# A PEER expert mixer on one Trainium2 core: the second row block's choices moved among the dense blocks, dot products among the queries, two rings for the query weights

## The chip, the cores and the metric

The kernel runs on one core of one Trainium2 chip. The core has five engines, each with its own in-order queue of instructions: TensorE (PE in the profile; its weight loads are listed apart as PEld), VectorE (DVE), ScalarE (ACT), GpSimd (POOL) and SyncE (SP), which here only issues DMAs. The metric is the device time of one execution in microseconds (us), lower is better; a kernel's time is the median of its runs. A profile shows one execution, and its span runs from the first to the last instruction.

## The reference

One decoding step of a hybrid layer: an input projection feeds an RWKV-7 head group and a sparse-attention head group, whose outputs are projected, added to the input and normed. Then comes the part that the change touches, a PEER mixer: for every token and each of 8 heads, two halves of a query are scored against 128 subkeys each, the best 16 of either half are combined, the best 16 of the combinations name 16 of 16384 experts, and each chosen expert adds its row of `v_tab`, weighted by a gate and by the gelu of the dot product of the token with the expert's row of `u_tab`. There are 256 prompt tokens and 32 sample tokens, D = 2048, all in float32.

```python
q = (xt @ wq).reshape(n, P_HEADS, 2, P_DKEY // 2)
s = jnp.einsum('nhcd,hckd->nhck', q, subkeys).astype(jnp.float32)
hv, hix = lax.top_k(s, P_TOPK)
cand = (hv[:, :, 0, :, None] + hv[:, :, 1, None, :]).reshape(n, P_HEADS, P_TOPK * P_TOPK)
cand_e = (hix[:, :, 0, :, None] * N_KEYS + hix[:, :, 1, None, :]).reshape(n, P_HEADS, P_TOPK * P_TOPK)
tv, tpos = lax.top_k(cand, P_TOPK)
expert = jnp.take_along_axis(cand_e, tpos, axis=-1)
gate = jax.nn.softmax(tv, axis=-1).astype(x.dtype)
h = jax.nn.gelu(jnp.einsum('cd,chkd->chk', xb, u_tab[eb]), approximate=False)
return jnp.einsum('chk,chkd->cd', gb * h, v_tab[eb])
```

## The kernel before

The kernel is written against a layer that records instructions in program order, allots tiles in on-chip memory, adds the semaphores, and orders each engine's queue by a planner: it simulates the run and lets each engine take, of the instructions that are ready in the simulation, the one that stands first in the program. So an instruction can be queued earlier than its place in the text, and what the planner took for ready is waited for on the chip. `tc.issue_after(x)` holds the instructions inside it behind `x` on the queue of `x`'s engine. Tiles come from pools that are stacked from the left and from the right end of the memory; a pool that is closed gives its place to later ones, whose tiles wait until the old tile there is no longer used. A tile name with `bufs=n` is a ring of n places.

The 256 prompt tokens are two row blocks of 128, `t` = 0 and 1. From the first norm on (lines 1716 to 1756), in program order:

- **Norm.** The rows X1 are normed, turned into `XT` for TensorE, multiplied and shifted, and written to DRAM as `X1D` by four DMAs of GpSimd (line 1752).
- **Query stage** (lines 1762 to 1857). For head `h` TensorE multiplies `XT` with the query weights of two column groups `c` (32 loads of 512 KB through one ring, `wraw`, of four tiles; line 1711), ScalarE copies the result to `QP`, TensorE scores both row blocks against the subkeys, and ScalarE copies the scores to `TB`, where four tiles take turns (line 1383). `choose` (line 1386) then finds the best on VectorE, with the sums of indices and a masked product (lines 1394, 1400, 1411) on GpSimd; `settle` reduces the masked product to 16 indices of experts, a head later, which GpSimd writes to `GI[t]`. Dot products of the 32 sample tokens (`late`, line 1556; two gathers of 512 KB a token) run in between on VectorE. At `h == 2` SP loads the first 896 columns of the normed rows back, `X1a[t]` (line 1829).
- **Dense blocks** (lines 1854 to 1876). The dot product of token and expert is split by columns. For the last 1152 columns TensorE forms all 128 x 128 experts' products in 128 blocks `i1`: nine float32 matmuls each, 18 instructions in the profile, on weights `ur` of 576 KB (ring of five), into five PSUM banks `ph`, from which ScalarE copies to `AW`. For the first 896 columns only the chosen experts are formed: per pair of row block and choice one gather of 448 KB by GpSimd into `rows` (ring of five) and one multiply-and-sum by VectorE into a column of `HD[t]` (line 1794), 256 in all, two a block in program order. These are the *dots*. `gates` (softmax of the chosen scores, an exponential on ScalarE) stands ahead of the blocks for both row blocks, and `table(0)`, which turns indices, gates and `HD` of the first row block for the next stage, at 152 dots.
- **Weigh stage** (lines 1879 to 2012), 64 steps that read `AW` and `TB`; `table(1)` stands at step 20. The ring `rows` also takes the sample tokens' gathers of this stage.
- **V stage** (line 2016 on), the weighted sum of the experts' rows of `v_tab`, then the last norm. The first load of its table, line 1971, stands at step 50 of the weigh stage.

## Time and profile before

| what | value |
|---|---|
| time, median of three runs (lowest to highest) | 2457.12 us (2453.75 to 2460.82) |
| the profiled execution's own time | 2451.44 us |
| its span | 2449.7 us |
| TensorE / VectorE / ScalarE / GpSimd busy, share of the span | 92% / 71% / 33% / 54% |
| mean granted TensorE clock | 0.95 |
| DMA over the span | 684.09 MB, mean 279 GB/s |

A row of the costliest groups reads: line, engine, operation, output<-input, shapes, count, then busy us and mean ns of one, then the engine's idle time ahead of them and what ended it. A row of the timeline reads: start and length in us, engine, line, operation, output<-input, shapes, count, and in brackets the idle time before it with what ended it; equal neighbours are merged. Matmuls overlap, so the mean duration of one is longer than the distance from one to the next. An SPq row in the view of waits gives what SP's queue waited for: us in total, times, the longest.

### The profile page before, as it was taken

The page shows a single profiled execution, that of the slowest core. Times are in us where ns is not written, and L with a number is a line of the kernel's source. Part 1 is how long each engine was busy: PE and PEld are TensorE (multiplying, and loading weights), DVE is VectorE, ACT ScalarE, POOL GpSimd, SP SyncE. Part 2 cuts the span into 40 slices and gives each one's busy share as a digit, 9 for nine tenths or more (in the row PEclk, how much of TensorE's full clock was granted, in tenths as well). Part 3 has the DMA queues.
Part 4 walks back from the last instruction along what each step waited for, and adds up shares of the span by engine and source line. Part 5 has one row for each costly group of instructions (what it writes and reads, how often), then busy time and mean ns, then how long its engine had stood idle before and what let it go on. Part 6 is the DMA issues. An engine that isn't in the chain of part 4 may idle for free.

```text
span 2449.7 us, 42718 instructions
## 1 busy us (share of the span) xinstructions
PE 2254.7 (92%) x15628; PEld 1886.4 (77%) x15628; DVE 1748.2 (71%) x3985; ACT 819.9 (33%) x1591; POOL 1332.6 (54%) x1419
## 2 busy tenths in 40 slices
PE   7989999997988997779989999998998999999996
PEld 7977898884645665568878888887777888887885
DVE  5789766555653456789955555556777799998888
ACT  4433223223431333220111111111777544444343
POOL 5678423233445003567757555666442688876762
PEclk9999999998996996999999999999999999999998
DMA  7887975448668984988499999998664799999994
GB/s 221 233 247 224 281 213 167 136 141 261 213 228 250 312 277 160 320 287 271 147 402 399 400 403 388 390 400 313 190 190 131 280 359 365 357 369 361 353 346 187
DMA packets 327602, 684.09 MB, mean 279 GB/s; under 512 B 82270, under 2 KB 200992, under 8 KB 326464
## 3 DMA queue, kind: packets, MB, share of 16 engines
q1 hardware_dynamic: 246176, 342.58, 42.1%
q0 software_dynamic: 81216, 338.78, 38.4%
q8 instruction: 123, 2.02, 0.3%
q14 instruction: 87, 0.71, 0.1%
HBM read 665.69 MB, written 23.88 MB: 281 GB/s over the span
## 4 chain that ended last, share of the span: by engine, by line
PE 51%; issue 13%; DVE 12%; POOL 11%; DMA 9%; ACT 2%; SPq 1%; POOLq 0%; DVEq 0%; ACTq 0%
PE pb L2066 20%; POOL rows L454 9%; PE pj L423 8%; PE pa L1660 3%; PE px L1904 3%; PE pa L1937 2%; DVE sr L1556 2%; PE p L1080 2%; PE pt L1896 2%; DMA co<-in_cache_cmp_kv,gidx 2%; PE ss L1497 1%; DMA rows<-in_peer_u_g,gi 1%; PE fs L1955 1%; DVE CA L477 1%; DMA co<-in_cache_sel_kv,sidx 1%
## 5 line engine op out<-in xcount | busy, mean ns | idle before, releaser
L1867 PE MATMUL ph<-Xfd,ur 128*128 128x256 f32 x2304 | 500.8, 380 | 10.1 <-DMA ur<-in_peer_u_t 9.7
L1867 PEld LDWEIGHTS ph<-Xfd,ur 128*128 128x128 f32 x2304 | 439.2, 191 | 71.0 <-issue 10.0
L454 POOL DMA_INDIRECT rq<-in_peer_v_g,gi x256 | 377.6, 1475 | 153.2 <-DVE fP L2039 88.4
L1794 DVE SCALAR_TENSOR_TENSOR rows<-rows,x1a 128x896 f32<-128x896 f32 x256 | 282.0, 1103 | 197.0 <-DMA rows<-in_peer_u_g,gi 195.9
L454 POOL DMA_INDIRECT rows<-in_peer_u_g,gi x256 | 293.1, 1145 | 184.8 <-DVE rows L1794 152.8
L423 PE MATMUL pj<-XH,wl 128*128 128x288 f32 (+1 forms) x752 | 232.2, 309 | 11.3 <-DVE wl L418 6.4
L423 PE MATMUL pj<-XH,wh 128*128 128x288 f32 (+1 forms) x752 | 230.4, 306 | 13.0 <-DVE ss L753 5.9
L2039 DVE SCALAR_TENSOR_TENSOR fP<-rq,ge,fP 128x640 f32<-128x640 f32 x254 | 223.7, 881 | 7.8 <-DMA rq<-in_peer_v_g,gi 5.5
L423 PE MATMUL pj<-XL,wh 128*128 128x288 f32 (+1 forms) x752 | 226.6, 301 | 0.0
L1868 ACT COPY AW<-ph 128x256 f32<-128x256 f32 x128 | 77.0, 609 | 405.9 <-PE ph L1867 400.2
L2066 PE MATMUL pb<-vl,ah 128*128 128x512 f32 (+1 forms) x768 | 207.0, 378 | 0.8
L2066 PE MATMUL pb<-vh,al 128*128 128x512 f32 (+1 forms) x768 | 205.3, 375 | 0.0
L2066 PE MATMUL pb<-vh,ah 128*128 128x512 f32 (+1 forms) x768 | 186.7, 378 | 13.4 <-ACT vh L2058 10.9
L416 ACT CAST wh<-wraw 128x512 fp32r<-128x512 f32 (+1 forms) x188 | 114.6, 616 | 224.1 <-PE pj L423 178.5
L2066 PEld LDWEIGHTS pb<-vh,ah 128*128 128x128 f32 x768 | 144.8, 195 | 35.7 <-ACT vh L2058 13.9
L477 DVE SCALAR_TENSOR_TENSOR CA<-co,wbc,CA 128x256 f32<-128x256 f32 x248 | 135.9, 586 | 49.7 <-DMA co<-in_cache_cmp_kv,gidx 49.7
L2066 PEld LDWEIGHTS pb<-vl,ah 128*128 128x128 f32 x768 | 144.9, 195 | 23.0 <-DVE vl L2059 3.8
L423 PEld LDWEIGHTS pj<-XH,wl 128*128 128x128 f32 (+1 forms) x752 | 144.4, 192 | 22.4 <-DVE wl L418 9.1
L2066 PEld LDWEIGHTS pb<-vh,al 128*128 128x128 f32 x768 | 145.0, 194 | 19.4
L423 PEld LDWEIGHTS pj<-XH,wh 128*128 128x128 f32 (+1 forms) x752 | 144.9, 193 | 19.4 <-DVE ss L753 6.4
L423 PEld LDWEIGHTS pj<-XL,wh 128*128 128x128 f32 (+1 forms) x752 | 144.9, 193 | 1.5 <-issue 1.2
L418 DVE TENSOR_TENSOR wl<-wraw,wh 128x512 fp32r<-128x512 f32 (+1 forms) x141 | 100.2, 720 | 40.0 <-ACT wh L416 39.8
(844 smaller groups left out, 4331.4 us busy)
## 6 DMA issues: line engine op xcount, KB each, us to landing
ur<-in_peer_u_t SPq DMA_DIRECT2D x128, 576.0 KB
wraw<-in_w_in SPq DMA_DIRECT2D x152, 256.0 KB
cw<-in_w_out SPq DMA_DIRECT2D x32, 512.0 KB
wraw<-in_w_out SPq DMA_DIRECT2D x32, 512.0 KB
wraw<-in_peer_wq SPq DMA_DIRECT2D x32, 512.0 KB
cw<-in_peer_wq SPq DMA_DIRECT2D x32, 512.0 KB
wraw<-in_w_in SPq DMA_DIRECT2D x64, 128.0 KB
co<-in_state_win_kv SPq DMA_DIRECT2D x16, 512.0 KB
```

The costliest lines, as they stand in the source:

```text
L416: sc.copy(wh[:, :, :n], w[:, :, :n])
L418: i_ = en.tensor_tensor(wl[:, :, :n], w[:, :, :n], wh[:, :, :n].bitcast(F32), OP.subtract)
L423: last[2] = pe.matmul(pb[:n, :nt], wi[:, k, :n], xi[(o + k) // 8][:, (o + k) % 8, :nt], start=(o + k == 0 and wi is wh and xi is xh), stop ...
L454: gp.indirect_dma_start(out=dst, out_offset=None, in_=rows_, in_offset=bass.IndirectOffsetOnAxis(ap=ix, axis=0))
L477: ve.scalar_tensor_tensor(d_, x_, w_, d_, op0=OP.mult, op1=OP.add)
L1660: pe.matmul(acc[t], xi[:, e, P * t:P * t + P], wi[:, e, :], start=(k == e == n_ == 0), stop=(k == 6 and e == 1 and n_ == 2))
L1794: i_ = ve.scalar_tensor_tensor(r_, r_, 1.0, X1a[t], op0=OP.mult, op1=OP.mult, accum_out=h_)
L1867: mm = pe.matmul(ph[:, :NPR], w[:, e, :], Xfd[:, e, :], start=(e == 0), stop=(e == NDB - 1))
L1868: return mm, sc.copy(AW[:, i1 // 64, :, i1 % 64], ph[:, :NPR])
L1904: pin(pe.matmul(px[:, 128 * e:128 * e + 128].rearrange("p (c j) -> p c j", c=2), oT[:, e, :], AW[:, :, 4 * u + e, :], start=True, stop=True))
L2039: ve.scalar_tensor_tensor(fP[t], r_, w_, fP[t], op0=OP.mult, op1=OP.add)
L2066: pe.matmul(acc[3 * t + q][:, :n_], wi[:, P * t:P * t + P], xi[:, 512 * q:512 * q + n_], start=(k == 0 and wi is ah and xi is vh), stop=(k ...
```

## The change

Five constants change: `NDW` (dots per head in the query stage) from 1 to 5, `NCB` = 10 is new, `ND` and `NDN` go.

- In the query stage `choose` runs for row block 0 alone. Its scores go to `TB[:, h % 4]`; those of row block 1 go to a new tile `S1` with a place for every head. From `h` = 3 on, five dots follow each head (30 in all) where one followed each of the last two.
- The choices of row block 1 are made by a new generator `choose_parts`, six parts a head, drawn among the dense blocks at six parts per ten blocks, behind the last dot so far on VectorE. All of its work is on VectorE, but for the copy of the indices to `GI[1]`, which is ScalarE's. `gates(1)` follows at block 80, `table(0)` moves to block 90.
- The dots that are left are spread evenly over the 128 blocks.
- Query weights come through two rings of four tiles, `wraw` and `wraw2`. The load of `X1a[0]` stands behind the 13th weight load on SP's queue, that of `X1a[1]` and the dense weights behind the last.
- `QP` is a ring of six tiles of one column group each. `rows` moves to a pool `rp` of its own with tiles of 896 columns, closed before the weigh stage, which has its own ring `rows`. The order of the pools on the left becomes `up`, `rp`, `dp` (with `S1`), `kc`, `kq`.

```diff
-NDW = 1
-ND = 1
-NDN = 8
+NDW = 5
+NCB = 10
...
-        S = TB[:, (2 * h + t) % 4].rearrange("p (a b) -> p a b", a=2) if t < 2 else pool([P, 2, P], "S")
+        S = (TB[:, h % 4], S1[:, h])[t].rearrange("p (a b) -> p a b", a=2) if t < 2 else pool([P, 2, P], "S")
...
+    def choose_parts(h, pool, S, TV):
+
+        HV, HI, HF = (pool([P, 2, 16], nm, ty) for nm, ty in (("HVb", F32), ("HIb", U32), ("HFb", F32)))
+        for c in range(2):
+            top16(S[:, c, :], HV[:, c, :], HI[:, c, :])
+            yield 1
+        for c in range(2):
+            ve.tensor_scalar(HF[:, c], HI[:, c], 1.0 if c else 1.0 * P, 0.0, op0=OP.mult, op1=OP.add)
+        CV, CE = (pool([P, NCAND], nm) for nm in ("CVb", "CEb"))
+        for dst, src in ((CV, HV), (CE, HF)):
...
+        yield 1
+        TI, TF = (pool([P, 16], nm, ty) for nm, ty in (("TIb", U32), ("TFb", F32)))
+        top16(CV, TV[:, h, :], TI)
+        ve.tensor_copy(TF, TI)
+        yield 1
+        hit = rp([P, UG], "rows", bufs=NRW)[:, :16 * NCAND].rearrange("p (a b) -> p a b", a=16)
+        ve.tensor_tensor(hit, iota[:, None, :NCAND].to_broadcast([P, 16, NCAND]),
+                         TF[:, :, None].to_broadcast([P, 16, NCAND]), OP.is_equal)
+        ve.tensor_tensor(hit, hit, CE[:, None, :].to_broadcast([P, 16, NCAND]), OP.mult)
+        yield 1
+        EF = pool([P, 16], "EFb")
+        ve.tensor_reduce(EF, hit, AX.X, OP.add)
+        sc.copy(GI[1][:, 16 * h:16 * h + 16], EF)
+        yield 1
...
-        w = wring()
-        sy.dma_start(w, w_q[:, 128 * c:128 * c + 128].rearrange("(k p) c -> p k c", p=P)[:, o:o + 8])
+        w = wring() if c == 0 or o else kq([P, 8, P], "wraw2", bufs=4)
+        wl_.append(sy.dma_start(w, w_q[:, 128 * c:128 * c + 128].rearrange("(k p) c -> p k c", p=P)[:, o:o + 8]).ins)
...
+    rp([P, UG], "rows", bufs=NRW)
+    S1 = dp([P, 8, 2 * P], "S1")
...
-        if h == 2:
-            for t in range(2):
+        if h in (3, 8):
+            with tc.issue_after(wl_[12 if h < 8 else -1]):
+                t = h // 8
                 sy.dma_start(X1a[t], X1D[P * t:P * t + P, :UG])
         if h:
             late_, hits = hits, []
-            for t in range(2):
-                chosen, hit = choose(t, h - 1, kc, S[t], TV[t])
-                hits.append(hit)
+            chosen, hit = choose(0, h - 1, kc, S[0], TV[0])
+            hits.append(hit)
...
-                if h > 6:
+                if h > 2:
                     dot(NDW, 16 * (h - 1), ahead=2)
...
-    for t in range(2):
-        gates(t, up, TV[t])
+    gates(0, up, TV[0])
...
-        sy.dma_start(w.rearrange("p k e -> p (k e)"), a["peer_u_t"][P * i1:P * i1 + P, :])
+        with tc.issue_after(wl_[-1]):
+            sy.dma_start(w.rearrange("p k e -> p (k e)"), a["peer_u_t"][P * i1:P * i1 + P, :])
...
+    later, early = seq(*(choose_parts(h, kc, S1[:, h].rearrange("p (a b) -> p a b", a=2), TV[1]) for h in range(8))), got[1]
     for i1 in range(P):
         mm, end = dense(i1)
-        n_ = ND + (i1 * NDN % 8 < NDN)
-        dot(min(max(P - got[1], 0) or n_, n_))
-        if got[1] == P + 24:
+        n_ = early + -(-(2 * P - early) * (i1 + 1) // P)
+        dot(n_ - got[1])
+        with tc.issue_after(last_dot[0].ins):
+            for _ in take(later, 6 * (i1 + 1) // NCB - 6 * i1 // NCB):
+                pass
+            if i1 == 8 * NCB:
+                for _ in later:
+                    pass
+                gates(1, up, TV[1])
+        if i1 == 8 * NCB + 10:
             with tc.issue_after(mm.ins), tc.issue_after(end.ins):
                 table(0)
     kc.close()
     dp.close()
+    rp.close()
...
+    x4p([P, 1024], "rows", bufs=NRW)
...
-    dot(2 * P - got[1])
```

More of the change, by code (lines that the diff above doesn't have):

```diff
@@ L1374, in scores @@
             if t < 2:
-                pe.matmul(pb[:, 128 * c:128 * c + 128], QP[:, 2 * h + c, P * t:P * t + P], SKT[:, 2 * h + c, :],
+                pe.matmul(pb[:, 128 * c:128 * c + 128], QP[2 * h + c][:, P * t:P * t + P], SKT[:, 2 * h + c, :],
                           start=True, stop=True)
@@ L1386, in choose @@
     def choose(t, h, pool, S, TV):
-        nb_ = 2 if t < 2 else 1
+        nb_ = 1
         HV, HI, HF = (pool([P, 2, 16], nm, ty, bufs=nb_) for nm, ty in (("HV", F32), ("HI", U32), ("HF", F32)))
@@ L1404, in choose @@
         TI, TF = (pool([P, 16], nm, ty, bufs=nb_) for nm, ty in (("TI", U32), ("TF", F32)))
-        hit = up([P, 1024], "rows", bufs=NRW) if t < 2 else pool([P, 1024], "cw", bufs=NCW)
+        hit = rp([P, UG], "rows", bufs=NRW) if t < 2 else pool([P, 1024], "cw", bufs=NCW)
         hit = hit[:, :16 * NCAND].rearrange("p (a b) -> p a b", a=16)
@@ L1412, in choose @@
         return i_, hit
+    def choose_parts(h, pool, S, TV):
[7 more added lines that the diff above has]
+        for dst, src in ((CV, HV), (CE, HF)):
+            o = 0
+            for i0, ni, w in CAND:
+                ve.tensor_tensor(dst[:, o:o + ni * w].rearrange("p (i j) -> p i j", i=ni),
+                                 src[:, 0, i0:i0 + ni, None].to_broadcast([P, ni, w]),
+                                 src[:, 1, None, :w].to_broadcast([P, ni, w]), OP.add)
+                o += ni * w
+        yield 1
[12 more added lines that the diff above has]
+        yield 1
     def settle(t, h, pool, hit):
@@ L1708, in query_load @@
     def query_load(c, o):
-        w = wring()
-        sy.dma_start(w, w_q[:, 128 * c:128 * c + 128].rearrange("(k p) c -> p k c", p=P)[:, o:o + 8])
+        w = wring() if c == 0 or o else kq([P, 8, P], "wraw2", bufs=4)
+        wl_.append(sy.dma_start(w, w_q[:, 128 * c:128 * c + 128].rearrange("(k p) c -> p k c", p=P)[:, o:o + 8]).ins)
         return w
+    wl_ = []
     wq_ = {(0, o): query_load(0, o) for o in (0, 8)}
@@ L1766, in hybrid_decode_step @@
     TV = [up([P, 8, 16], f"TV{t}") for t in range(2)]
-    up([P, 1024], "rows", bufs=NRW)
     xa_ = up([P, 2 * UG], "x1a")
@@ L1770, in hybrid_decode_step @@
     TB = up([P, 4, NPR], "TB")
-    dp, kc, kq = (Pool(nm, "left") for nm in ("dp", "kc", "kq"))
+    rp, dp, kc, kq = (Pool(nm, "left") for nm in ("rp", "dp", "kc", "kq"))
+    rp([P, UG], "rows", bufs=NRW)
+    S1 = dp([P, 8, 2 * P], "S1")
     dp([P, NDB, P], "ur", bufs=NUR)
@@ L1774, in hybrid_decode_step @@
     SKT = kq([P, 16, P], "SKT")
-    QP = kq([P, 16, NPR], "QP")
     dots = [(t, s_) for t in range(2) for s_ in range(P)]
-    got, rows_ = [0, 0], {}
+    got, rows_, last_dot = [0, 0], {}, []
     def fetch(upto):
@@ L1783, in fetch @@
             t, s_ = dots[i]
-            rows_[i] = up([P, 1024], "rows", bufs=NRW)[:, :UG]
+            rows_[i] = rp([P, UG], "rows", bufs=NRW)
             gather(rows_[i], a["peer_u_g"], GI[t][:, s_:s_ + 1])
@@ L1796, in dot @@
                 tc.keep_in_program_order(i_)
-            got[1] = i + 1
+            got[1], last_dot[:] = i + 1, [i_]
     def table(t):
@@ L1802, in table @@
         for q, (op_, v_) in enumerate(((OP.logical_shift_right, 7), (OP.bitwise_and, 127))):
-            ii = up([P, P], "ii", I32, bufs=4)
+            ii = up([P, P], "ii", I32, bufs=2)
             iff = ii.bitcast(F32)
@@ L1815, in hybrid_decode_step @@
     for h in range(9):
-        S = []
+        S, QP = [], {2 * h - 2 + c: q_ for c, q_ in enumerate(QN)} if h else {}
+        QN = [kq([P, NPR], "QP", bufs=6) for c in range(2)]
         for c in (2 * h, 2 * h + 1):
@@ L1823, in hybrid_decode_step @@
                         pe.matmul(pb[:, :NPR], w[:, k, :], XT[:, o + k, :], start=(o + k == 0), stop=(o + k == 15))
-                last_ = sc.copy(QP[:, c, :], pb[:, :NPR])
+                last_ = sc.copy(QN[c % 2], pb[:, :NPR])
             if h and c == 2 * h:
                 S = [scores(t, h - 1, kc, QP, SKT, "pb") for t in range(2)]
-        if h == 2:
-            for t in range(2):
+        if h in (3, 8):
+            with tc.issue_after(wl_[12 if h < 8 else -1]):
+                t = h // 8
                 sy.dma_start(X1a[t], X1D[P * t:P * t + P, :UG])
@@ L1949, in smp_fetch @@
         for q in range(2):
-            sr[j, q] = up([P, 1024], "rows", bufs=NRW)
+            sr[j, q] = x4p([P, 1024], "rows", bufs=NRW)
             gather(sr[j, q], vh2, ig[q][:, j:j + 1])
```

## The prediction

> **What bounds the kernel now.** I read the page's costliest groups first, then TensorE's timeline from the first query matmul to the first matmul of the next stage, then what SP's queue waited for.
>
> ```profile
> L1867 PE MATMUL ph<-Xfd,ur 128*128 128x256 f32 x2304 | 500.8, 380 | 10.1 <-DMA ur<-in_peer_u_t 9.7
> ```
> ```profile
> L1794 DVE SCALAR_TENSOR_TENSOR rows<-rows,x1a 128x896 f32<-128x896 f32 x256 | 282.0, 1103 | 197.0 <-DMA rows<-in_peer_u_g,gi 195.9
> ```
> ```profile
> 1052.18 17.53 PE L1823 MATMUL pj<-XT,wraw 128*128 128x256 f32 x80 [1.89 <-ACT XT L1736]
> ...
> 1089.78 1.22 PE L1375 MATMUL pb<-SKT,QP 128*128 128x128 f32 x4 [4.05 <-ACT QP L1824]
> ...
> 1104.38 13.29 PE L1823 MATMUL pj<-XT,wraw 128*128 128x256 f32 x48 [4.97 <-DMA wraw<-in_peer_wq]
> ...
> 1132.65 13.98 PE L1823 MATMUL pj<-XT,wraw 128*128 128x256 f32 x64
> ...
> 1147.36 13.98 PE L1823 MATMUL pj<-XT,wraw 128*128 128x256 f32 x64
> ...
> 1184.86 27.36 PE L1867 MATMUL ph<-Xfd,ur 128*128 128x256 f32 x126
> 1212.69 11.92 PE L1867 MATMUL ph<-Xfd,ur 128*128 128x256 f32 x54 [0.47 <-ACT AW L1868]
> 1234.27 255.35 PE L1867 MATMUL ph<-Xfd,ur 128*128 128x256 f32 x1170 [9.66 <-DMA ur<-in_peer_u_t]
> ```
> ```profile
> 1497.23 198.73 PE L1867 MATMUL ph<-Xfd,ur 128*128 128x256 f32 x920
> ...
> 1700.28 0.48 PE L1809 MATMUL pb<-CT,hd 128*128 128x128 f32 x1 [3.99 <-DVE rows L1794]
> ...
> 1703.27 2.07 PE L1904 MATMUL px<-AW,oT 128*128 128x128 f32 x8 [0.68 <-ACT oT L1898]
> ```
>
> TensorE is the bound of this stretch, and it is nearly gapless. A head of the query stage costs 1147.36 − 1132.65 = 14.71 us. A dense matmul costs 198.73 / 920 = 0.216 us, so a dense block (18 of them) costs 3.89 us. Eight heads and 2304 dense matmuls need 117.7 + 497.7 = 615.4 us. From 1052.18 that would end at 1667.6; it ended at 1695.96. So 28 us were lost: 4.05 + 4.97 + 0.47 + 9.66 = 19.2 us in four gaps, the rest to a lower clock behind them. Another 7.3 us pass until the first matmul of the weigh stage, 3.99 of them waiting for the last dot product. VectorE has gaps too: its 256 dots wait 195.9 us for gathered rows. In the last 400 us of the dense stage the DMA engines are full:
>
> ```profile
> 1295.00:1695.00 400.00, 400.00 (x1857) 352.09 (x1856) 234.40 (x427) 63.15 (x104) 247.54 (x214) 1.00 1.01 393
> ```
>
> (The columns: stretch and length, then busy time and instructions of TensorE, its weight loads, VectorE, ScalarE and GpSimd, then TensorE's granted clock, the DMA share and GB/s.) So two chains run side by side through the dense blocks and end 4 us apart: TensorE's, and the dots' behind the DMA. Only shortening both moves the end.
>
> **The change part by part.** The causes of the gaps are in what SP's queue and ScalarE waited for; the last two rows are stretches with a low clock:
>
> ```profile
> SPq L1971 <- POOL gi L1418: 19.1, 1, 19.1
> SPq L1829 <- DMA x1d<-x: 11.6, 2, 7.4
> ```
> ```profile
> 1086.62 0.65 ACT L1383 COPY TB<-pb 128x256 f32<-128x256 f32 x2 [12.17 <-DMA x1d<-x]
> ```
> ```profile
> 1079.54 0.59 POOL L1752 DMA_DIRECT2D x1d<-x  x1
> ```
>
> ```profile
> 1105.00:1120.00 15.00, 15.00 (x62) 12.85 (x61) 15.00 (x66) 1.30 (x4) 11.67 (x22) 0.84 0.87 276
> ```
> ```profile
> 1234.00:1240.00 6.00, 5.73 (x15) 4.64 (x16) 3.51 (x7) 0.00 (x0) 2.89 (x4) 0.54 1.02 411
> ```
>
> *Normed rows' load (line 1829).* SP is in order, and it sat 11.6 us on the two X1a loads while query weights stood behind them. The change puts X1a[0] behind the 13th weight load and X1a[1] behind the last, and doubles the ring to eight tiles. Eight tiles are two heads, 29 us of TensorE. The 4.97 us go, and with them the slow clock behind them: 62 matmuls in 15 us where 15 / 0.216 gives 69, so 7 × 0.216 = 1.5 us. **−6.5 us.** If the cover failed it would cost these 6.5 again.
>
> *First scores.* ScalarE stood 12.2 us because TB lies on the old X1 rows, whose write to DRAM had to land first; the query copy behind it cost TensorE 4.05 us. By the tiles' sizes, TB moves off those rows, but the new S1 falls on X1's second block, written out last, issued at 1079.54; had that landed as late as 1089, the wait would have been some 2.5 us longer. Between −4.05 (the copies of queries are put first) and +2.5. I take **0**.
>
> *First load of the V stage (line 1971).* It was hoisted to where SP waited 19.1 us for the last choice; the dense weights behind it came late: 9.66 us, then 6 us at clock 0.54 (15 matmuls where 28 fit, 13 × 0.216 = 2.8 us). After the change this tile lies, by the sizes, over Xfd and the choice tiles, both in use until late in the dense blocks, so it can't be issued there. With the 0.47 us: **−12.9 us**; if it is hoisted badly again, none of it.
>
> *Choices on VectorE.*
>
> ```profile
> 1104.21 0.86 DVE L1363 MAX8 HV<-TB 128x8 f32<-128x128 f32 x4
> ...
> 1111.54 2.02 DVE L1409 TENSOR_TENSOR rows<-CT,TF 128x864 f32<-128x864 f32 x2
> 1113.48 2.01 DVE L1417 TENSOR_REDUCE EF<-rows 128x16 f32<-128x864 f32 x2
> ```
> ```profile
> 1211.46 0.69 ACT L1425 ACTIVATE ge<-ge 128x128 f32<-128x128 f32 x2 [18.03 <-DVE ge L1424]
> 1212.06 1.02 ACT L1868 COPY AW<-ph 128x256 f32<-128x256 f32 x2
> 1213.10 1.28 ACT L1562 ACT_TABLE_LOAD   x1
> ```
> ```profile
> L1400 DVE TENSOR_TENSOR CV<-HV 128x16 f32<-128x16 f32 (+3 forms) x80 | 9.5, 158 | 0.0
> ```
>
> Two choices take 1113.48 − 1104.21 = 9.27 us and two reductions 1.92. One of each, 5.6 us a head, leaves the query stage; 30 dots of 1.10 us come in over six heads, 5.5 us a head. So where sample dots, choice and dots meet (heads 3 to 6) VectorE's head stays as long as it is, and for each dot that waits for its row it grows; the others get shorter. I keep the end of its queries, 1211.46 now, near 1207. The gate's exponential waits for that, and ScalarE's copies of the dense banks stand behind it. TensorE will reach dense block 0 at 1184.86 − 6.5 = 1178, fill two copied blocks and five banks, 7 × 3.89 = 27 us, and stop at 1205 until ScalarE is let go: between 0 and 6 us (if VectorE ends at 1211 as now). I take **+2.4 us.** In the dense blocks one choice costs 5.6 us plus what GpSimd did: the product, as wide as the comparison (1.0), and seven small ones (9.5 / 80 = 0.12 us in a row of them, 0.158 alone). That is 7.4 us; with its twenty-odd steps one behind the other, not two heads interleaved as here, perhaps 9.8. So 59 to 78 us in all.
>
> *The dots' chain.* 226 dots remain. One takes 1.10 us and waits 195.9 / 256 = 0.77 for its row: 1.87 us, 423 us from 1207. While a choice holds VectorE, up to five gathers go on in flight, so of its 68 us (the middle) I count 0.4: 27. The dots end near 1657. TensorE ends near 1178 + 497.7 + 2.4 = 1678. So the dots fall off the path, the 3.99 us wait at the weigh stage's start goes: **−3.7 us** (between 0 and −5.4). The DMA agrees: 128 × 576 KB and 226 × 448 KB are 179 MB, 456 us at 393 GB/s, under 498. The weigh stage's own ring lies over `rows`, `S1` and `ur`, free by then, and is read only from its fourth step on: 0, or one gather's landing at the stage's start.
>
> *Gates twice.* The second exponential stands behind a Gelu and before another, two table loads of 1.28 us. ScalarE is busy 63 of 400 us there and hides one; the other stands at the weigh stage's first Gelu: **+1.3 us.** The Trainium skill (ScalarE: Activation LUTs, What ACT_TABLE_LOAD costs) counts 2.66 us for a switch, a drain beside the load; the row above shows 1.28 for the load alone, and no run here shows the drain. By it the sum would be 1.4 us higher.
>
> Sum: −6.5 + 0 − 12.9 + 2.4 − 3.7 + 1.3 = −19.4 us. The profiled execution took 2451.44 us (span 2449.7), the median of the three runs is 2457.12; I carry the difference over: **2437.7 us**.
>
> **The rivals.**
>
> *The dots still end last.* If VectorE's choices add fully, 1207 + 423 + 78 = 1708, where TensorE got the last dot at 1700 before: the dense stage gains nothing and loses little, 2449 to 2466, say 2457. For it: serial small instructions, and the mask takes one of five row buffers. Against: 195.9 us of gaps to fall into.
>
> *DMA bound in the queries.*
>
> ```profile
> L454 POOL DMA_INDIRECT sr<-in_peer_u,ig x16 | 21.2, 1324 | 16.7 <-DVE sr L1556 12.9 <-issue 1.7 <-DVE HI L1364 1.5
> L454 POOL DMA_INDIRECT sr<-in_peer_u,gi x15 | 17.8, 1188 | 5.8 <-DVE sr L1556 3.5 <-DVE TB L1365 1.2 <-issue 1.1
> ```
>
> From 1052 to 1178 must come 28 of the 32 weight tiles and these 31 sample gathers, 512 KB each, 30 rows of 448 KB, five dense blocks and some 4 MB besides: 52 MB. At 393 GB/s that is 132 us instead of 126. The row from 1105 moved 276 at a share of 0.87, 317 at a full one; half way between, 353, it is 147 us: 21 us lost, 2459. Against: the weights come by their own queue with 29 us of lead; it is the gathers that would wait. The Trainium skill (DMA: Bandwidth & Descriptors, Specifications) gives a core some 358 GB/s from HBM, which would make as much of it and hold the dense blocks at 500 us; the trace disagrees, with 393 over 400 us.
>
> *Slower: ScalarE held by VectorE.* The second block's indices are written by ScalarE, in order with the copies that free TensorE's five banks. It decides once VectorE is more than five blocks (19.4 us) behind the place where a copy was queued. At its worst: copies in program order, head 7 at block 80, 1178 + 311 = 1489; VectorE there after 142 dots (266 us) and 78 us, 1551. TensorE then stops 62 − 19.4 = 43 us, and the kernel takes 2437.7 + 43 = 2481; half of it, 2459, is no change; I say 2472. Against it, the planner's own order:
>
> ```profile
> L1794 DVE SCALAR_TENSOR_TENSOR rows<-rows,x1a x123: 1080/1093/2656, 1203.1 to 1450.0; 128x896 f32<-128x896 f32 x123
> ```
> ```profile
> L1864 SPq DMA_DIRECT2D ur<-in_peer_u_t x80: 327/328/619, 1089.1 to 1489.6; - x80
> ```
> ```profile
> 1490.31 0.85 SPq L2004 DMA_DIRECT2D x1a<-in_ln_b  x2
> ```
>
> The load at 1490.31 needs dot 128. It was queued behind the 80th dense weight, block 75; the chip had dot 123 at 1450, so 128 near 1460, 30 us or eight blocks sooner. The planner thinks VectorE later than it is, so ScalarE's copies should be queued late enough.
>
> **How the numbers follow.** Forecast 2437.7, chance 0.56, its own range 2425 (first scores' 4.05 gone, the other 3 us of slow clock, no hold, 1.7 more at the weigh) to 2449. Dots last 0.15, DMA bound 0.10, both near no change; held ScalarE 0.12; gaps elsewhere 0.07, split evenly. Two in ten lie outside 2424 to 2462. A measurement of this kernel can tell about 0.3% (7.4 us) from no change: faster 0.56 + 0.10 from the milder ends of the others = 0.66; same 0.19; slower 0.15.
>
> **What would show it.** Right: no gap for wraw near 1100 nor for ur near 1225; TensorE without gaps from its first dense block on, its end near 1678; the last dot before it; the first weigh matmul some 4 us behind. Wrong: ScalarE waiting for EF with TensorE waiting for AW (held); TensorE waiting for hd at the end (dots last); gaps for wraw or ur at a full DMA share. Most would be upset by an order on SP or ScalarE that the planner chose otherwise.

## The result and the profile after

| | before | after the change |
|---|---|---|
| median, same chip | 2457.09 us (6 runs, 2452.88 to 2463.98) | 2437.05 us (6 runs, 2432.69 to 2450.29) |
| ratio to before, 95% interval | | 0.9928 (0.9900 to 0.9955) |
| profiled execution, its span | 2451.44, 2449.7 us | 2450.29, 2448.5 us |

The change makes the kernel some 18 us faster (0.72%; between 0.45 and 1.0%). The two profiled executions alone don't show that: the changed kernel's is the slowest of its six runs. Its first query matmul starts at 1072.43 us, 20.25 us later than before, although all five queues carry the same instructions up to there. Over all profiles of this study that start lies between 1052 and 1079 us. So the stretches behind it are compared, each counted from its own first query matmul.

TensorE's timeline of the changed kernel, from the first query matmul to the first matmul of the weigh stage (start, busy us, engine, line, operation; in brackets the idle time before it and what ended that):

```profile
1072.43 7.17 PE L1855 MATMUL pj<-XT,wraw 128*128 128x256 f32 x32 [1.22 <-ACT XT L1767]
...
1087.56 1.19 PE L1374 MATMUL pb<-SKT,QP 128*128 128x128 f32 x4 [7.95 <-DMA SKT<-in_subkeys_t]
1089.27 16.34 PE L1855 MATMUL pj<-XT,wraw 128*128 128x256 f32 x64 [0.52 <-DMA wraw<-in_peer_wq]
...
1202.26 353.70 PE L1899 MATMUL ph<-Xfd,ur 128*128 128x256 f32 x1638
...
1556.24 143.91 PE L1899 MATMUL ph<-Xfd,ur 128*128 128x256 f32 x666
...
1702.30 0.33 PE L1840 MATMUL pb<-CT,hd 128*128 128x128 f32 x1 [1.82 <-DVE rows L1825]
1703.53 0.63 PE L1937 MATMUL pt<-CT,oo 128*128 128x128 f32 x4 [0.90 <-DVE oo L1933]
1704.87 2.08 PE L1945 MATMUL px<-AW,oT 128*128 128x128 f32 x8 [0.72 <-ACT oT L1939]
```

The page's groups of the same kernel:

```profile
L1899 PE MATMUL ph<-Xfd,ur 128*128 128x256 f32 x2304 | 497.6, 379 | 0.0
...
L1825 DVE SCALAR_TENSOR_TENSOR rows<-rows,x1a 128x896 f32<-128x896 f32 x256 | 278.8, 1097 | 136.2 <-DMA rows<-in_peer_u_g,gi 135.5
```

The waits of 4.05 us (for a query copy), 4.97 us (for query weights) and 9.66 us (for dense weights) are gone. The dense group's idle time went from 10.1 to 0.0 us. A wait of 7.95 us for the subkeys is new, and the wait for hd, the dots' results, has shrunk from 3.99 to 1.82 us: in this profile the dots still come last.

| from, to | before | after | the change, profiled again |
|---|---|---|---|
| first query matmul, first dense one | 132.7 | 129.8 | 130.9 |
| dense blocks | 511.1 | 497.9 | 497.9 |
| their end, first weigh matmul | 7.3 | 4.7 | 2.2 |
| the three together | 651.1 | 632.4 | 631.1 |
| last dot done, from the first query matmul | 648.0 | 629.8 | 628.4 |

The gain of the stretch, 18.7 and 20.0 us, is what the medians show. Most of it, 13.2 us, lies in the dense blocks. The rest of the kernel, 746.4 us from the first weigh matmul to the end of the span before, is 743.6 and 746.0 us.

### The profile page after: what moved, and what is told of

Same layout as the page of the kernel before. It is cut to its first block, busy times and chain, and to the rows that moved or that the text cites. A ratio compares the mean times of both kernels' runs of the same rounds, so it can differ in the third digit from the quotient of the medians.

```text
span 2448.5 us, 42558 instructions
## 1 busy us (share of the span) xinstructions
PE 2255.8 (92%) x15628; PEld 1888.4 (77%) x15628; DVE 1762.0 (72%) x4049; ACT 823.4 (34%) x1601; POOL 1332.6 (54%) x1347
## 3 DMA queue, kind: packets, MB, share of 16 engines
q8 instruction: 123, 2.02, 0.3%
## 4 chain that ended last, share of the span: by engine, by line
PE 29%; DMA 9%; DVE 8%; issue 7%; POOL 4%; ACT 1%; POOLq 0%; DVEq 0%; SPq 0%; ACTq 0%
PE pb L2107 20%; DMA rows<-in_peer_u_g,gi 8%; POOL rows L453 4%; PE px L1945 3%; DVE rows L1825 2%; PE pa L1978 2%; PE pj L1855 2%; PE pt L1937 1%; PE fs L1997 1%; DVE sr L1586 1%; DVE vl L2100 1%; DMA wraw<-in_peer_wq 0%; ACT vh L2099 0%; PE pa L1690 0%; DVE cw L1586 0%
## 5 line engine op out<-in xcount | busy, mean ns | idle before, releaser
L453 POOL DMA_INDIRECT rows<-in_peer_u_g,gi x256 | 313.3, 1224 | 189.3 <-DVE rows L1825 119.0
```

The costliest lines, as they stand in the source:

```text
L453: gp.indirect_dma_start(out=dst, out_offset=None, in_=rows_, in_offset=bass.IndirectOffsetOnAxis(ap=ix, axis=0))
```

## The experiments

**Theory.** Two chains run side by side and end together: TensorE's, and that of the dots (indices, gathers, VectorE). The change shortens both by about as much, TensorE's by an order on SP that leaves no gap, the dots' by starting 30 of them among the queries. **Rivals:** the gain is TensorE's gaps alone; or the dots alone; and of the dots: the DMA sets their pace, or VectorE does. Ratios are to the kernel before on the same chip, with 95% intervals; the chips differ (medians of before from 2452 to 2471 us).

### How much a profile's stretches vary: `change_again`

The changed kernel, unaltered.

> The changed kernel unaltered, as the measure of what one profile's stretches are worth. Theory (the stretch from the first query matmul to the first weigh matmul doesn't depend on when it starts): dense blocks start at 129 to 132 us, end at 627 to 630, last dot 628 to 632, first weigh matmul 630.5 to 633.5 us behind the first query matmul, one wait of VectorE of 11 to 17 us for the second gates' exponential; ratio to before 0.990 to 0.996. Rival, the stretch varies as the whole time does: first weigh matmul outside 629 to 636, and the differences of 2 to 5 us read between kernels mean nothing.

Ratio 0.9925 (0.9891 to 0.9959). Dense blocks 130.9 to 628.8, last dot 628.4, first weigh matmul 631.1: within 1.5 us of the first profile. So differences of 4 us and more between stretches are read below as real, smaller ones with care: this rests on two profiles. VectorE's one long wait was 20.33 us here, longer than I expected.

### TensorE's gaps alone: `sp_only`

```diff
-        if h == 2:
-            for t in range(2):
-                sy.dma_start(X1a[t], X1D[P * t:P * t + P, :UG])
+        if h in (3, 8):
+            with tc.issue_after(wl_[12 if h < 8 else -1]):
+                t = h // 8
+                sy.dma_start(X1a[t], X1D[P * t:P * t + P, :UG])
...
+        with tc.issue_after(wl_[-1]):
+            ul_.append(sy.dma_start(w.rearrange("p k e -> p (k e)"), a["peer_u_t"][P * i1:P * i1 + P, :]).ins)
...
+            with tc.issue_after(ul_[-1]):
+                rows_load(0)
```

> The kernel before, with the change's order on SP alone: the X1a loads behind the 13th and the last query weight load, dense weights behind the last of these, the V stage's first load behind the last dense weight. Choices, dots and rings as before. Two chains that both must get shorter: TensorE's gaps at the query weights (4.97 us) and at the dense weights (9.66 us) go and the dense blocks end some 625 us behind the first query matmul (before: 643.8), but the 254 dots in the dense blocks end as before, near 648, so TensorE waits 15 to 22 us for hd and the first weigh matmul stands at 648 to 655 (before: 651.1; after the change: 632.4); 2453 to 2460 us, no change. Rival, TensorE's gaps were all there was to gain: first weigh matmul near 633, wait for hd under 5 us, 2438 us.

Ratio 0.9988 (0.9957 to 1.0019): no change, as the theory says. TensorE's timeline of `sp_only`:

```profile
1073.20 20.99 PE L1824 MATMUL pj<-XT,wraw 128*128 128x256 f32 x96 [0.66 <-ACT XT L1737]
...
1232.99 267.48 PE L1871 MATMUL ph<-Xfd,ur 128*128 128x256 f32 x1224 [6.85 <-ACT AW L1872]
...
1715.93 0.47 PE L1810 MATMUL pb<-CT,hd 128*128 128x128 f32 x1 [8.79 <-DVE rows L1795]
...
1718.92 2.08 PE L1908 MATMUL px<-AW,oT 128*128 128x128 f32 x8 [0.68 <-ACT oT L1902]
```

Both DMA gaps are gone with SP's order alone. Of the 10.2 us by which the dense blocks end earlier (633.6 in place of 643.8), about half is given back at once: TensorE now waits 8.79 us for the last dot, and the first weigh matmul stands at 645.7 (expected 648 to 655), only 5.4 us better, as much as the last dot itself comes earlier here (642.7 in place of 648.0). The 6.85 us in the middle were not expected. ScalarE's queue explains them:

```profile
ACT ge L1425 <- DVE ge L1424: 19.0, 1, 19.0
```

ScalarE stood 19.0 us at both blocks' gate exponentials, with the copies of the dense banks queued behind. (The columns: in all, times, longest.) That is the kind of hold that the prediction priced at 2.4 us for the changed kernel.

### The early dots: `two_early_dots`

```diff
-NDW = 5
+NDW = 1
...
-                if h > 2:
+                if h > 6:
                     dot(NDW, 16 * (h - 1), ahead=2)
```

> The changed kernel with 2 dots among the queries in place of 30. Theory (from 1250 us on the dots go at the pace of the DMA, 1.96 us each, and an early dot is worth only what VectorE could not have done instead before 1250): VectorE is free near 1210 of the profiled run after the change, does some 20 dots by 1250 and has 22 done there in place of 28, so the last dot comes 6.5 x 1.96 = 13 us later: first weigh matmul 640 to 652 us behind the first query matmul (now 632.4), wait for hd 10 to 20 us, 2445 to 2455 us. Rival, each dot saves its full 1.96 us: 28 x 1.96 = 55 us later, 2490. Rival, the early dots buy nothing: 632, 2437.

Ratio 1.0040 (1.0003 to 1.0077): with two early dots the change is not faster than the kernel before at all. TensorE's dense blocks end as in the changed kernel (628.8), and then it waits:

```profile
1718.80 0.47 PE L1840 MATMUL pb<-CT,hd 128*128 128x128 f32 x1 [26.41 <-DVE rows L1825]
...
1721.84 2.07 PE L1945 MATMUL px<-AW,oT 128*128 128x128 f32 x8 [0.72 <-ACT oT L1939]
```

The first weigh matmul stands at 658.6. I expected 640 to 652: the last dot comes 25.7 us later, twice what the theory gave the 28 dots and half of what the rival did. But that is no price per dot. In both kernels VectorE stands for ScalarE late in the dense blocks (the section on VectorE's holds has more), until 478.1 us behind the first query matmul in the changed kernel and until 485.9 here:

```profile
1549.13 0.36 DVE L1836 TENSOR_SCALAR ii<-gi 128x128 int32<-128x128 int32 x2 [22.00 <-ACT gi L1441]
```

Behind it 94 dots are left in place of 82. They take 169.6 us in place of 151.7; with the 7.8 us by which the hold ends later, that is the 25.7.

Together with `sp_only` this shows that the gaps alone are not the gain: with SP's order and no early dots nothing measurable is left, whether the choices have moved or not. The dots alone, with SP's old order, were not run. The profile before bounds what they could give: its dense blocks end at 643.8, and where TensorE waits for no dot the first weigh matmul comes some 2 us behind (1.6 in `no_holds`, 2.2 in `change_again`). That would be 646 in place of 651.1, by this estimate some 5 of the 18.7 us.

### What sets the dots' pace: `no_second_choices`, `half_rows`

```diff
-            for _ in take(later, 6 * (i1 + 1) // NCB - 6 * i1 // NCB):
-                pass
             if i1 == 8 * NCB:
-                for _ in later:
-                    pass
-                gates(1, up, TV[1])
+                gates(1, up, TV[0])
...
+    gp.tensor_copy(GI[1], GI[0])
```

> The changed kernel without the second row block's choices: its expert numbers and gates are copies of the first block's; scores, dots and gathers stay. Theory, the dots are held by the DMA: 8 choices of VectorE fewer move the last dot less than 10 us earlier than now (now 629.8 us behind the first query matmul), and TensorE's wait for hd goes at most. Rival, VectorE holds the dots and the choices add their 59 to 78 us: the last dot stands near 560 to 590.

The kernel leaves the second block's choices out and takes the first block's. The last dot stands at 626.7, 3 us earlier, as the theory says, but not for its reason. 200 us of the dense blocks, first of the changed kernel, then of this one (the third busy time is VectorE's; at the end clock, DMA share, GB/s):

```profile
1300.00:1500.00 200.00, 200.00 (x928) 176.05 (x928) 153.13 (x426) 31.36 (x57) 117.97 (x99) 1.00 0.99 381
```
```profile
1296.00:1496.00 200.00, 200.00 (x928) 176.05 (x928) 119.61 (x218) 31.70 (x52) 108.44 (x109) 1.00 1.02 403
```

GpSimd's count is that of the gathers: 99 and 109, so 2.02 us a dot with the choices and 1.83 without. The DMA moves 381 GB/s with the choices and 403 without, at shares of 0.99 and 1.02, so a share of 0.99 was not its limit. What hid the gain is a longer hold later on, 31.69 us:

```profile
1547.12 0.29 DVE L1456 TENSOR_REDUCE sm<-ge 128x8 f32<-128x128 f32 x1 [31.69 <-ACT ge L1455]
```

So this run's small shift is no sign that the choices cost nothing: they cost 0.19 us a dot while they last.

```diff
-            gather(rows_[i], a["peer_u_g"], GI[t][:, s_:s_ + 1])
+            gather(rows_[i][:, UG // 2:], a["peer_u_g"].rearrange("n (q c) -> (n q) c", q=2), GI[t][:, s_:s_ + 1])
...
+            i_ = ve.scalar_tensor_tensor(v2(r_), r_[:, None, UG // 2:].to_broadcast([P, 2, UG // 2]), 1.0, v2(X1a[t]),
+                                         op0=OP.mult, op1=OP.mult, accum_out=h_)
...
+                with tc.issue_after(ul_[-1]):
+                    sy.dma_start(x_[r_, :], X1D[NPR:NT, c_])
```

> The changed kernel with gathers of half rows (448 elements, 224 KB a dot in place of 448); the dot still goes over 896 elements, the gathered ones twice, so VectorE's work is unchanged. Theory, the dots are held by the DMA: they then go at VectorE's pace, 226 x 1.18 + 70 = 337 us, and the last one stands 515 to 560 us behind the first query matmul (now 629.8); TensorE's wait for hd goes and the first weigh matmul stands at 629 to 631. Rival, VectorE holds them: the last dot stays within 20 us of where it is.

With half the bytes the last dot stands at 551.6, 78 us earlier, inside the range of the theory that the transfers hold the dots. But the dots don't go at VectorE's pace, as it said. Here is a stretch behind the last choice in which TensorE does not stop:

```profile
1496.00:1590.00 94.00, 94.00 (x432) 82.34 (x430) 64.93 (x121) 15.03 (x26) 73.80 (x60) 0.99 0.81 264
```

That is 60 dots at 1.57 us, against 1.83 for full rows without choices and 1.18 expected, with VectorE busy 65 of 94 us and the DMA's share at 0.81. So the bytes are part of what holds the dots; what else does is not shown. The other half of the expectation fell: the first weigh matmul stands at 718, since the planner, which now believes the dots quicker, queued ScalarE's and SP's work on them too early (ScalarE's first copy of indices stands behind 13 dense copies in place of 18, the last behind 59 in place of 89). ScalarE, at the indices that VectorE has to deliver, and TensorE, at the banks that ScalarE has to copy:

```profile
1279.71 0.20 ACT L1441 CAST gi<-EFb 128x16 int32<-128x16 f32 x1 [27.84 <-DVE EFb L1440]
...
1341.93 0.21 ACT L1441 CAST gi<-EFb 128x16 int32<-128x16 f32 x1 [22.20 <-DVE EFb L1440]
1370.01 0.20 ACT L1441 CAST gi<-EFb 128x16 int32<-128x16 f32 x1 [19.96 <-DVE EFb L1440]
...
1400.78 0.20 ACT L1441 CAST gi<-EFb 128x16 int32<-128x16 f32 x1 [19.64 <-DVE EFb L1440]
```
```profile
1280.47 30.43 PE L1902 MATMUL ph<-Xfd,ur 128*128 128x256 f32 x126 [9.81 <-ACT AW L1903]
...
1342.69 26.16 PE L1902 MATMUL ph<-Xfd,ur 128*128 128x256 f32 x108 [4.17 <-ACT AW L1903]
1370.77 29.15 PE L1902 MATMUL ph<-Xfd,ur 128*128 128x256 f32 x126 [1.93 <-ACT AW L1903]
1401.55 8.04 PE L1902 MATMUL ph<-Xfd,ur 128*128 128x256 f32 x36 [1.62 <-ACT AW L1903]
```

Read in pairs, ScalarE's wait less TensorE's gap is 18.03, 18.03, 18.03 and 18.02 us. That is what the banks absorb, 4.6 dense blocks. (A fifth long wait, of 25.71 us, falls together with a stop of TensorE for ur.) And SP:

```profile
SPq L2049 <- DVE rows L1826: 49.6, 1, 49.6
```

A load into X1a's place stood 49.6 us, until the last dot was done, with dense weights behind it; an earlier one had stood until 1409.48, for the last dot of the first block. Behind the two, TensorE waited 37.97 and 8.07 us for ur, 46.0 in all, beside 26.1 us for the banks.

### The normed rows' load: `x1a_early`

```diff
-        if h in (3, 8):
-            with tc.issue_after(wl_[12 if h < 8 else -1]):
-                t = h // 8
-                sy.dma_start(X1a[t], X1D[P * t:P * t + P, :UG])
+        if h == 2:
+            with tc.issue_after(wl_[9]):
+                for t in range(2):
+                    sy.dma_start(X1a[t], X1D[P * t:P * t + P, :UG])
```

> The changed kernel with both X1a loads asked for at the third head and held behind the 10th query weight load, as they stood before the change (now: behind the 13th and the last). Theory (SP, in order, stands at X1a until the norm's rows have landed, some 40 us behind the first query matmul, and weights queued behind it come late): a gap of TensorE for wraw of 5 to 16 us near 35 to 50 us behind the first query matmul (now 0.52 us), the dense blocks start later by as much, first weigh matmul 636 to 648 us behind the first query matmul (now 632.4). Rival, the ring of eight tiles covers it by itself: wait for wraw under 1 us, 632 +- 3.

A miss: the longest wait for wraw is 1.57 us, the first weigh matmul stands at 631.2, as in the changed kernel. SP held each load for 1.7 us only, and showed no wait for the rows' write here. The two edits of the term, the place of the load and the ring of eight, are not separated by this run: with the ring of eight and the lost 8 us at the subkeys, the early place costs nothing in the one profile.

### TensorE's wait at the queries' start: `late_scores`, `preloaded`

```diff
-            if h and c == 2 * h:
-                S = [scores(t, h - 1, kc, QP, SKT, "pb") for t in range(2)]
+            if h and c == 2 * h + (h == 1):
+                with tc.issue_after(mq.ins):
+                    S = [scores(t, h - 1, kc, QP, SKT, "pb") for t in range(2)]
```

> The changed kernel with head 0's scores behind column group 3's matmuls (now half of them behind group 0's), so that TensorE has 48 more matmuls to do while the subkeys' load lands. Theory (two chains end together): the wait of 7.95 us for SKT shrinks to under 1.5 us and the dense blocks end 5 to 8 us earlier behind the first query matmul (now 627.7), but the dots end as now (629.8) or up to 3 us earlier, so TensorE waits 5 to 10 us for hd, and the first weigh matmul stands at 629 to 633 (now 632.4): 2434 to 2438 us, ratio 0.992. Rival, the 7.95 us come out in full: first weigh matmul near 625, 2429 us.

Ratio 0.9910 (0.9883 to 0.9937). The wait for the subkeys is gone, and a longer one stands in its place:

```profile
1097.67 22.44 PE L1855 MATMUL pj<-XT,wraw 128*128 128x256 f32 x96 [11.08 <-DMA wraw<-in_peer_wq]
```

The dense blocks end at 629.0 and the first weigh matmul stands at 631.6: nothing gained. So not the place of the scores, but what the DMA has brought by then, sets TensorE's start. The third weight tile (first of the second ring) is loaded behind the subkeys, 4.8 us after the first query matmul in the changed kernel. The next run moves it into the old ring:

```diff
-        w = wring() if c == 0 or o else kq([P, 8, P], "wraw2", bufs=4)
+        w = wring() if c < 2 or o else kq([P, 8, P], "wraw2", bufs=4)
...
+                    if (c, o) == (2, 0):
+                        with tc.issue_after(wl_[-1]):
+                            sy.dma_start(SKT, a["subkeys_t"])
```

> The changed kernel with column group 1's first half in the old ring (so that the first four weight tiles load before the queries start; the second ring lies over rows that the norm still uses), the subkeys' load behind the fifth weight tile, and head 0's scores behind column group 3. Theory (the 8 to 11 us that TensorE waits at the start of the queries, for the subkeys or with late scores for the third weight tile, come from loads that the second ring lets start only 4 us behind the first query matmul): waits for SKT and wraw under 4 us in all, the dense blocks start 121 to 125 us behind the first query matmul (now 129.8; 131.2 with late scores) and end at 619 to 623, the dots end as now, 626 to 630, TensorE waits 4 to 10 us for hd, first weigh matmul 629 to 632. Rival, the DMA is full there whatever the order: waits of 7 us and more stay, in another place.

Ratio 0.9968 (0.9944 to 0.9992), and the rival's sign is there. TensorE runs 33 us with no wait over 0.7 us, and then waits 8.32 us:

```profile
1112.12 5.80 PE L1857 MATMUL pj<-XT,wraw 128*128 128x256 f32 x16 [8.32 <-DMA wraw<-in_peer_wq]
```

In the run with the same edits further down, these are the 20 us from the first query matmul and the 20 behind them (same columns as above):

```profile
1057.00:1077.00 20.00, 19.27 (x88) 16.70 (x89) 20.00 (x17) 6.42 (x19) 18.24 (x14) 1.00 0.97 309
1077.00:1097.00 20.00, 13.21 (x66) 11.37 (x64) 14.61 (x44) 3.58 (x7) 13.16 (x19) 0.94 1.07 365
```

The DMA's share is 0.97 and 1.07 while TensorE waits. SP's issues of these loads tell the same (shortest, median and longest, in ns):

```profile
L1741 SPq DMA_DIRECT2D wraw<-in_peer_wq x32: 367/1698/8858, 795.2 to 1155.5; - x32
```

An issue that takes 0.37 us when nothing holds it took 8.86 us at 1080.23. So what fits is that the loads come no faster than the transfers allow. Three orders of them have moved the wait, and none made it smaller than 7.9 us. But all three use two rings. `sp_only`, with one ring of four, moves as much in the same two stretches, and TensorE gets its weights; its one wait over 0.7 us before the dense blocks is for a query copy:

```profile
1073.20:1093.20 20.00, 20.00 (x93) 17.62 (x94) 20.00 (x17) 5.95 (x17) 18.24 (x14) 1.00 0.96 311
1093.20:1113.20 20.00, 15.71 (x74) 13.66 (x73) 10.87 (x55) 4.23 (x9) 10.12 (x17) 0.91 1.08 364
```
```profile
1110.17 1.22 PE L1375 MATMUL pb<-SKT,QP 128*128 128x128 f32 x4 [4.29 <-ACT QP L1825]
```

Its dense blocks start 125.6 us behind the first query matmul, against 129.8 in the changed kernel, 129.7 here and 128.4 in `both_chains`. So a full DMA does not cost TensorE 8 us whatever the order. That loads asked for early through the second ring delay the one that TensorE needs next would fit; no run tests it. That the first weigh matmul came 10 us later than in the changed kernel (642.3) is another thing: the dots ended at 639.2, behind a wait of VectorE of 20.50 us.

### VectorE's holds: `gate_split`, `split_and_late`, `no_holds`

In the changed kernel VectorE has one long wait among the dense blocks:

```profile
1550.50 0.29 DVE L1456 TENSOR_REDUCE sm<-ge 128x8 f32<-128x128 f32 x1 [11.69 <-ACT ge L1455]
```

It subtracts the maxima for the second gates, and then stands in order at their sum until ScalarE has done the exponential, which is queued behind copies that TensorE paces. The dots' queue stands with it. ScalarE's queue there, the copy being that of the 89th dense block:

```profile
1548.23 0.60 ACT L1900 COPY AW<-ph 128x256 f32<-128x256 f32 x1 [3.28 <-PE ph L1899]
...
1548.86 1.28 ACT L1455 ACT_TABLE_LOAD   x1
1550.16 0.31 ACT L1455 ACTIVATE ge<-ge 128x128 f32<-128x128 f32 x1
```

So TensorE sets when the hold ends. In the second profile of the same kernel VectorE came earlier and stood longer:

```profile
1542.14 0.29 DVE L1456 TENSOR_REDUCE sm<-ge 128x8 f32<-128x128 f32 x1 [20.33 <-ACT ge L1455]
```

Behind the first query matmul VectorE came at 466.4 and 458.9 us in the two profiles, and at 447.6 without the second choices; it was let go at 478.1, 479.2 and 479.3. What VectorE gains before the hold it waits there, and the dots' end depends on how many are left behind it (82, 82 and 81).

```diff
             if i1 == 8 * NCB:
                 for _ in later:
                     pass
-                gates(1, up, TV[1])
+                ve.tensor_tensor(GE1, TV[1], TV[1][:, :, 0:1].to_broadcast([P, 8, 16]), OP.subtract)
+                ex_ = sc.activation(GE1, GE1, AF.Exp)
+            if i1 == 8 * NCB + 8:
+                sm8 = up([P, 8], "sm8")
+                ve.tensor_reduce(sm8, GE1, AX.X, OP.add)
...
```

> The changed kernel with the second gates cut in two: difference and exponential at block 80 as now, sum, reciprocal and product at block 88, so that VectorE doesn't stand for the exponential. Theory (the hole of 11.69 us at 1550 is a wait in VectorE's queue in which gathers stop too, and the dots' chain ends last by some 2 us): no such wait, the last dot 8 to 12 us earlier, TensorE's wait for hd (1.82 us) gone, and only these 2 us come out at the end: first weigh matmul 629 to 631 us behind the first query matmul (now 632.4), 2435 us, ratio to before 0.992. Rival, the dots are held by the DMA and catch the hole up: last dot within 3 us of now, wait for hd 1 to 3 us. Rival, the dots alone set the end: 9 to 11 us faster.

Ratio 0.9925 (0.9899 to 0.9952); the last dot stands at 633.3, no earlier, and the first weigh matmul at 636.4 (expected 629 to 631). That looks like the rival, but VectorE's timeline shows that the hold has only passed to what stood behind it:

```profile
1553.65 0.36 DVE L1836 TENSOR_SCALAR ii<-gi 128x128 int32<-128x128 int32 x2 [14.78 <-PE pb L1838]
```

The planner had queued the second table's shifts early. They need the tiles `ii`, of which the change left two in place of four, and TensorE reads the first table's out of them only at block 90. Both edits, `gate_split` and `late_scores`, together:

> Both edits of the two runs before. Theory: TensorE gets 7 us and the dots' chain 8 to 12 us shorter, so both come out: first weigh matmul 621 to 626 us behind the first query matmul (now 632.4), no wait for hd over 1 us, 2427 to 2431 us, ratio to before 0.988 to 0.990. Rival, the dots are held by the DMA and catch the hole up: 629 to 633, as with late scores alone.

Ratio 0.9915 (0.9884 to 0.9946), first weigh matmul at 630.6, VectorE's wait for `ii` 14.11 us: the expected 621 to 626 was missed, since neither edit had done its part. So the shifts were moved too:

```diff
+        if i1 == 110:
+            late_dot = last_dot[0]
...
-            ve.tensor_scalar(ii, GI[t], v_, None, op0=op_)
-            ve.tensor_copy(iff, ii)
+            with tc.issue_after((late_dot if t else chosen).ins):
+                ve.tensor_scalar(ii, GI[t], v_, None, op0=op_)
+                ve.tensor_copy(iff, ii)
```

> The changed kernel with the second gates cut in two as before, and the second table's shifts and casts on VectorE (its tiles are a ring of two since the change, and stood 14.78 us for TensorE's transposes of the first table) held behind the dot of block 110. Theory: VectorE has no wait over 4 us any more between 1250 us and the last dot; in the hold the DMA went on for five rows and lost only some 4 to 6 us, so the last dot stands 623 to 627 us behind the first query matmul (now 629.8, with the gates cut alone 633.2), TensorE's end (628 to 630) sets the time, wait for hd 0, first weigh matmul 630 to 632 (now 632.4): no more than 2 us of gain. Rival, the hold's whole 12 to 15 us come off the dots' chain: last dot 615 to 620. Rival, nothing: last dot 629 or later.

Now the last dot comes at 620.4, 8.0 to 9.4 us earlier than in the two profiles of the changed kernel, and 9.2 us before TensorE's end. (First and last start of the dots; one takes 1.1 us.)

```profile
L1825 DVE SCALAR_TENSOR_TENSOR rows<-rows,x1a x256: 1068/1092/2276, 1151.1 to 1692.7; 128x896 f32<-128x896 f32 x128
```

That is nearly the rival's 615 to 620, more than the 3 to 7 us that I gave it: 9.4 us against a hold of 11.69 in the first profile, 8.0 against 20.33 in the second. The time hardly follows, for TensorE is now last: first weigh matmul at 631.3, ratio 0.9913 (0.9888 to 0.9939).

### Both chains: `both_chains`

The edits of `no_holds` and of `preloaded` together.

> The edits of the two runs before together. Theory: TensorE's dense blocks end 619 to 623 us behind the first query matmul and the last dot stands at 620 to 626, so the first weigh matmul stands at 623 to 629 (now 632.4), 3 to 9 us better, ratio to before 0.988 to 0.991. Rival, the dots don't follow: 629 to 632, ratio as the change's own.

```profile
1098.27 5.24 PE L1858 MATMUL pj<-XT,wraw 128*128 128x256 f32 x16 [8.05 <-DMA wraw<-in_peer_wq]
...
1685.40 1.16 PE L1958 MATMUL px<-AW,oT 128*128 128x128 f32 x8 [0.74 <-ACT oT L1952]
```

The first weigh matmul stands at 627.9, 3.2 to 4.5 us before the changed kernel's, at the small end of the expected 3 to 9. The dots end 11 us before TensorE (615.3 and 626.3), and TensorE's dense blocks, without a gap, can't end earlier while 8.05 us are lost to the weights. Ratio 0.9915 (0.9891 to 0.9939), expected 0.988 to 0.991; median 2433.3 us. It beats the kernel before; that it beats the changed kernel (0.9928 and 0.9925) is what the trace suggests and what these times can't tell.

## Why the prediction was right, and where it was not

The forecast, −19.4 us, stands beside −20.0 us in the medians, and −18.7 and −20.0 us in the stretch. The mechanism was right in its main step; that the sum is met within a microsecond is in part luck, since the queries gave 3.6 to 4.8 us less than their terms, and two costs that did not come (2.4 + 1.3) are 3.7 us the other way. By its steps:

- **First load of the V stage: right.** −12.9 predicted, −13.2 measured in the dense blocks, both profiles alike. The load is issued at the end of the dense blocks now, as predicted, and `sp_only` shows the gap gone with SP's order alone.

```profile
1700.23 0.33 SPq L2013 DMA_DIRECT2D v__17765<-in_peer_v  x1
```

- **Normed rows' load and first scores: too large.** −6.5 and 0 predicted, −2.9 and −1.7 measured from the first query matmul to the dense blocks. Both old waits did go. What the step left out is that the planner takes half of head 0's scores a head earlier (behind 32 matmuls, before behind 96), and what the second ring does to the loads there: in each of the three orders with two rings TensorE waits some 8 to 11 us (7.95 for the subkeys, 11.08, 8.32 and 8.05 for weights). That is like the "DMA bound in the queries" rival in a small place, where I had said that only the gathers would wait; but `sp_only` shows the same DMA load without such a wait.
- **Hold of ScalarE at the gate's exponential: +2.4 predicted, 0 measured.** ScalarE waited 11.59 us, and TensorE had no gap: five blocks were copied when the wait began, where the step counted two. Five banks were taken for 19.4 us; `half_rows` shows 18.03.
- **The dots fall off the path: wrong.** They were to end at 1657, 20 us before TensorE; they ended 2.1 us behind it in one profile and 0.4 us before it in the other. The term, −3.7, became −2.6 and −5.1 all the same. Two steps failed. One is "30 dots come in ... I keep the end of its queries ... near 1207": counted from the first query matmul, 30 dots were to be done by 154.8, and the 30th started at 177.3 and 175.6. The other is the sum 423 + 27 behind it, which has no term for VectorE standing at the second gates. That hold, not the 30 dots, sets the end: VectorE is let go at 478.1 and 479.2 us, whenever it came, and the 82 dots left take 1.85 and 1.82 us each. So it is luck that the 450 us of the sum are 452.5 and 452.8 measured. They are made up otherwise: 226 dots at 1.83 us, the pace without choices, are 414; the choices add 0.19 us to each of the 146 dots that run among them (from 1250 to 1545 us at 2.02 us), 28 us, about the predicted 27; and the hold adds the remaining 10 (`no_holds`: 442.5 from the 30th dot to the last). Without the hold the late 30 dots do show: the last one at 620.4 in `no_holds`, where the prediction's 1657 is 604.8 behind the first query matmul.
- **Table loads: +1.3 predicted, nothing measured.** The second one stands at the weigh stage's first Gelu, as predicted, but from the first weigh matmul to the V stage's first it takes 213.2 us, and 213.4 before.

```profile
1712.03 1.28 ACT L1960 ACT_TABLE_LOAD   x1
1713.33 0.21 ACT L1960 ACTIVATE E<-E 128x8 f32<-128x8 f32 x1
```

The Gelu starts 1.30 us behind the load's start. The drain that the Trainium skill (ScalarE: Activation LUTs, What ACT_TABLE_LOAD costs) counts beside the load does not show in this trace.

Of the rivals, the held ScalarE did not come, but the reason given against it was false. "The planner thinks VectorE later than it is" holds for the kernel before; in the changed one VectorE was the later one in the first heads:

```profile
1285.85 0.20 ACT L1441 CAST gi<-EFb 128x16 int32<-128x16 f32 x1 [12.82 <-DVE EFb L1440]
1321.79 0.20 ACT L1441 CAST gi<-EFb 128x16 int32<-128x16 f32 x1 [9.95 <-DVE EFb L1440]
1358.76 0.20 ACT L1441 CAST gi<-EFb 128x16 int32<-128x16 f32 x1 [8.07 <-DVE EFb L1440]
1391.88 0.20 ACT L1441 CAST gi<-EFb 128x16 int32<-128x16 f32 x1 [2.31 <-DVE EFb L1440]
```

12.82 us is 5 us under what the banks absorbed in `half_rows`, and that run shows the mechanism at work where the wait is longer.

Why the early dots are late was not tried. From 1202 to 1250 us the DMA's share is 0.79, TensorE is full and VectorE busy for 37 of 48 us; among the queries only two rows are fetched ahead, five in the dense blocks. A chain of waits between VectorE and GpSimd fits that, but no run here shows it.

## What to carry to other kernels

Where two chains end together, price both: SP's order alone, and this change without its early dots, were worth nothing that could be measured. An in-order queue that waits takes all that stands behind it along, and when such a wait is removed, the next instruction in the queue may wait as long; look for it before saying that the time was caught up elsewhere. Where another engine sets the end of such a wait, what is gained before it is only waited longer. And a planner's order is part of the kernel: a run that makes one thing faster in its eyes can move instructions on other queues to where they hold everything up.

## What the runs showed of the hardware

- Five banks absorbed 18.03 us of ScalarE's waiting for indices in `half_rows`, to within 0.01 us in four cases (a dense block takes 3.89 us). At the gates of `sp_only`, where ScalarE had copied only two blocks, they absorbed less: a wait of 19.0 us left a gap of 6.85.
- A DMA share of 0.99 is no sign of a full limit: 381 GB/s at 0.99 with the choices, 403 at 1.02 without, in the same 200 us of the same loop. The Trainium skill (DMA: Bandwidth & Descriptors, Specifications) gives a core some 358 GB/s from HBM; this trace disagrees, with both numbers above it.
- The same instructions up to the query stage took between 1052 and 1079 us in the profiles (1072 and 1063 in the two of the changed kernel), a spread wider than the whole effect of this change.
